# A hybrid pooling and attention backbone on one core: the pool layer's first stage with pinned VectorE and ScalarE orders

## The chip, the cores and the metric

The kernel runs on one core of a Trainium2 chip. A core has a tensor engine (TensorE, PE) that multiplies matrices and writes to PSUM, a vector engine (VectorE, DVE), a scalar engine (ScalarE, ACT), a small general engine (GpSimd, POOL) and a sync engine (SyncE, SP), whose queue here issues every DMA. Each engine works through its own instructions in their order and waits at one whose inputs are not there.

The metric is the device time of one execution in microseconds. One further execution was recorded by the hardware profiler; its views are called the profile, or the trace.

## The reference

A backbone of two layers over 512 latent tokens (with 256 context tokens beside them), width 1024, float32. Layer 0 mixes tokens by centred mean pooling, layer 1 by attention; an MLP with squared ReLU follows each. What matters here is the beginning, the pool half of layer 0:

```python
def ada_mods(cond, w, b):
    m = (jax.nn.silu(cond) @ w + b)[..., None, :]
    return jnp.split(m, N_MOD, axis=-1)          # SH1, SC1, GT1, SH2, SC2, GT2

def pool_mixer(h, w_pool, pool_scale):           # h = rms_norm(x) * g * (1 + SC1) + SH1
    for g, w in enumerate((2, 4, 8, 16)):        # 4 groups of 256 channels
        mean = (jnp.take(csg, hi, axis=1) - jnp.take(csg, lo, axis=1)) / cnt
        diff = (mean - hf[..., sl]).astype(h.dtype)
        outs.append(diff @ w_pool[g])
    return jnp.concatenate(outs, axis=-1) * pool_scale

x = x + gt1 * rms_norm(y_lat, g_mix_post[i])
m_lat = sq_relu_mlp(modulate(rms_norm(x, g_mlp_pre[i]), sh2, sc2), w_mlp_in[i], w_mlp_out[i])
x = x + gt2 * rms_norm(m_lat, g_mlp_post[i])
```

The same is done for the context tokens with their own conditioning vector. The conditioning matrix of a layer, w_ada, is 1024 x 6144 float32; attention later scales q and k by the gains g_q and g_k.

## The kernel before

Tokens stand in six tiles of 128 rows (four latent, two context, `NT` = 6), channels in eight blocks of 128 (`KT` = 8). Float32 operands of the large matmuls are split into a high part that TensorE takes at its fast rate and a low rest, and three products (high x high, high x low, low x high) are added in PSUM.

The first stage, up to the MLP's first long run of matmuls, is made of these pieces; the names are functions in the code.

- `rows_a`, `rows_b`: RMS norm of each token tile; ACT squares, POOL takes the root, DVE scales into `acc`.
- `band_mm`, `band_ev`: the pooling means less identity as matmuls with a banded matrix, into PSUM (`psm` latent, `psc` context). Channel blocks 0 to 3 are copied to two SBUF tiles (`stage`), blocks 4 to 7 stay in PSUM.
- Conditioning, in fourteen items (`CONDITIONING`): a wide item covers 512 columns of one of the six vectors and takes two loads of 1 MB from w_ada, a narrow one covers 256 and takes one load, twenty loads in all. `ada_mm` loads and multiplies (eight matmuls whose four column groups of 32 hold partial sums, tile `psada`), and in the same step DVE transposes the rows in blocks of 32. For a wide item the transposed rows go into the loaded tile itself (`raw[:, 0, :]`). `ada_sel` then turns and sums them with small matmuls (`sel`), and DVE adds the bias and forms the scale vector (`avec`) or the negative of the shift (`minus`). The loads use four slots (pool `rawe`).
- `pool_weights`, `pool_scaled`, `split`: the 1 MB of pool weights is loaded, the 1024 values of pool_scale are copied by DMA to all 128 partitions, DVE multiplies them in, and one whole-tile cast (ACT) and subtraction (DVE) make high and low part.
- `centred(k)`: for one channel block, ACT makes the high part of mean x scale (latent, then context), DVE the low part. This needs SC1 and SH1 of that block.
- `pool_a`, `pool_ms`, `pool_b`: the pool matmuls of a token tile (6 per group, 24 in all, tile `pspool`), the mean square, and the product with the gate.
- `gate_rows`: GT1 times a gain is spread over the partitions by matmuls with the identity (`psg`), in two halves.
- `norm_r`, `norm_s`, `norm_c`, `turn0`, `mod0`, `Inner.part`: residual, second norm, transposes to channel-major, modulation with SC2 and SH2, and the first MLP matmuls (`psin`).

What sets the order: each call stands in a list with a time (`st.at(time, function, ...)`), and the list is run in order of these times. What the engines then execute is decided by a planner of the language, which may move instructions between its costs, except for those that are pinned. Pinned instructions of an engine stay in program order among themselves. The class `Kept` pins everything that goes through it while its switch is on. Before the change only TensorE goes through `Kept`, up to time 50.4 of the list; the loads of `raw_load` on SP are pinned by `raw_load` itself. In the profile every instruction that is pinned by `Kept` has line 65.

Two further lines matter. `head_gains` (line 986) loads g_q and g_k for the attention, spread over all partitions, and multiplies one of them by a constant on DVE. It is called from the MLP's block 4, far behind the first stage, but nothing pins it, and the planner issued both DMAs among the first on SP, with the multiply on DVE between the transposes of the first two conditioning items:

```python
        sy.dma_start(grow[:, 0, :], g_q[0].partition_broadcast(P))
        sy.dma_start(grow[:, 1, :], g_k[0].partition_broadcast(P))
        ve.tensor_scalar(out=grow[:, 0, :], in0=grow[:, 0, :], scalar1=float(HD) ** -0.5, ...)
```

Of the kernel before, what the change touches and what calls it, by code (L numbers as in the profile page):

```python
# [17 lines left out]
P = 128  # L18
# [50 lines left out]
def backbone(ctx: ExitStack, tc, x, ctx_in, w_ada, w_pool, pool_scale, w_qkv, g_q, g_k, w_o, w_mlp_in,  # L69
             w_mlp_out, vecs, rope, band, out):  # L70
    nc = tc.nc
    ordered = [False]
    sy, ve, sc, gp, te = nc.sync, nc.vector, nc.scalar, nc.gpsimd, Kept(tc, nc.tensor, ordered)
# [133 lines left out]
    sy.dma_start(vec, vecs[:, 0:160])  # L207
    sc.activation(cond[:, :, 0:2].rearrange("p k c -> p c k"), given.rearrange("p (c k) -> p c k", k=KT),
# [5 lines left out]
    def ada_mm(i, m, j, w=2):  # L214
        ps = psB.tile([P, 512], F32, tag="b", name="psada")
        kn = 2048 // (w * P)
        for z in range(KT // kn):
            raw = raw_load(w_ada[i, m, j + z]).rearrange("p (k n) -> p k n", n=w * P)
            for k in range(kn):
                at = kn * z + k  # L220
                q = 32 * (at % 4)
                te.matmul(ps[q:q + 32, 0:w * P], cond[:, at, :], raw[:, k, :], start=(at < 4), stop=(at >= 4))
        rows = raw[:, 0, :] if w > 2 else small.tile([P, 256], F32, tag="rows", name="rows", bufs=3)
        ve.transpose(rows, ps[:, 0:w * P])
        rowsd[i, m, j] = ps, rows, w
# [53 lines left out]

    def ada_at(st, t, i, m, j, w=2):  # L280
        st.at(t, ada_mm, i, m, j, w)
        st.at(t + 1, ada_sel, i, m, j)
# [136 lines left out]
    def band_ev(k, q, on_act):  # L419
        if k not in stage:  # L420
            z = rawp.tile([P, 2048], F32, tag="raw", name="stage")
            stage[k] = z[:, 0:2 * TOK].rearrange("p (u n) -> p u n", n=TOK), z[:, 2 * TOK:]
        t0, ln = SEGS[q]
        (sc.copy if on_act else ve.tensor_copy)(stage[k][0][:, :, t0:t0 + ln], (lat, con)[q][k])
        if q:
            for u in range(2):
                means[k + u] = [stage[k][0][:, u, t0:t0 + ln] for t0, ln in SEGS]
# [9 lines left out]
    def centred(k):  # L437
        pm = means.pop(k)
        for ci, (t0, ln) in enumerate(SEGS):
            hi, lo, m = hH[:, k, t0:t0 + ln], hL[:, k, t0:t0 + ln], pm[ci][:, 0:ln]  # L440
            sa = avec[0][0][:, k, ci:ci + 1]
            sc.activation(hi, m, AF.Identity, scale=sa, bias=minus[:, k, ci:ci + 1])
            ve.scalar_tensor_tensor(out=lo, in0=m, scalar=sa, in1=hi, op0=ALU.mult, op1=ALU.subtract)
# [7 lines left out]
    def pool_weights():  # L451
        wraw = raw_load(w_pool, rawp)
        w4 = wraw.rearrange("p (g k n) -> p g k n", k=2, n=256)
        for h, (_, spare) in enumerate(stage.values()):
            sy.dma_start(spare, pool_scale[0, 512 * h:512 * h + 512].partition_broadcast(P))
        pw.extend((wraw, wpH, wpL))

    def pool_scaled():
        w4 = pw[0].rearrange("p (g k n) -> p g k n", k=2, n=256)
        for h, (_, spare) in enumerate(stage.values()):  # L460
            ve.tensor_tensor(out=w4[:, 2 * h:2 * h + 2], in0=w4[:, 2 * h:2 * h + 2],
                             in1=spare.rearrange("p (g n) -> p g n", n=256).unsqueeze(2).broadcast_to([P, 2, 2, 256]),
                             op=ALU.mult)
# [245 lines left out]
    for t in range(NT):  # L709
        st.at(4.6 + 1.3 * t, rows_a, t)  # L710
        st.at(6.8 + 1.3 * t, rows_b, t)
# [9 lines left out]
    for t, z in enumerate((8.6, 9.9, 11.3, 13, 14.6, 18.4)):  # L721
        st.at(z, band_mm, t, range(4))
    for q, k, z in ((0, 0, 14.3), (0, 2, 14.3), (1, 0, 19.6), (1, 2, 19.6)):
        st.at(z, band_ev, k, q, k == 0)
    for k in (4, 6):
        z = 16.1 if k == 4 else 23.4
        st.at(z - 0.1, band_open, k)
        for t in range(NL):
            st.at(z + t / 10, band_mm, t, (k, k + 1))
        for t in range(NL, NT):  # L730
            st.at((25.6 if k == 4 else 27) + t / 10, band_mm, t, (k, k + 1))
# [8 lines left out]
    for h in range(2):  # L740
        for ci in range(2):
            st.at((44.8, 49.6)[h] + (0.1, 0)[ci], gate_rows, 0, GT1, ci, (h,))
    order = (4, 5, 0, 1, 2, 3)
    st.at(34.5, pool_a, 4, (0, 1), True)
    st.at(36.7, pool_a, 4, (2,))
    st.at(37.8, pool_a, 5, (0, 1, 2))
    st.at(40.4, pool_a, 4, (3,))
    st.at(40.5, pool_a, 5, (3,))
    for n, t in enumerate(order):
        b = 50.5 + 2.9 * n  # L750
        if n > 1:
            st.at((44.9, 52.6, 55.6, 58.4)[n - 2], pool_a, t)
        st.at(max(b - 0.5, 41.5 + 1.5 * n), pool_ms, t)
# [678 lines left out]
```

## Time and profile before

| | |
|---|---|
| median of 3 runs | 1183.19 us (1181.87 to 1183.25) |
| profiled execution | 1181.75 us, its span 1180.0 us |
| PE busy | 1140.9 us, 97% of the span |
| DVE busy | 938.0 us, 79% |
| ACT busy | 635.1 us, 54% |
| POOL busy | 65.8 us, 6% |
| bytes moved by DMA | 147.84 MB, mean 125 GB/s |
| granted TensorE clock, mean | 0.993 |

Times in the profile are microseconds from the start of the span. A row of the order of time has the start, the time to the end of the last of its instructions, engine, line, operation, result <- operands by name, shape and count; in brackets the idle time of the engine before it, and what ended that. Matmuls overlap, so a busy PE is not a PE at its peak. A DMA's row on SP is its issue, not the transfer.

### The profile page before, as it was taken

The page shows a single profiled execution, that of the slowest core. Times are in us where ns is not written, and L with a number is a line of the kernel's source. Part 1 is how long each engine was busy: PE and PEld are TensorE (multiplying, and loading weights), DVE is VectorE, ACT ScalarE, POOL GpSimd, SP SyncE. Part 2 cuts the span into 40 slices and gives each one's busy share as a digit, 9 for nine tenths or more (in the row PEclk, how much of TensorE's full clock was granted, in tenths as well). Part 3 has the DMA queues.
Part 4 walks back from the last instruction along what each step waited for, and adds up shares of the span by engine and source line. Part 5 has one row for each costly group of instructions (what it writes and reads, how often), then busy time and mean ns, then how long its engine had stood idle before and what let it go on. Part 6 is the DMA issues. An engine that isn't in the chain of part 4 may idle for free. (4 is left out here: it accounts for less than half of the span.)

```text
span 1180.0 us, 15950 instructions
## 1 busy us (share of the span) xinstructions
PE 1140.9 (97%) x6168; PEld 988.1 (84%) x6168; DVE 938.0 (79%) x1536; ACT 635.1 (54%) x1079; POOL 65.8 (6%) x120
## 2 busy tenths in 40 slices
PE   6699999999999999999999999999899999999997
PEld 5469889899889988998887889998888888888886
DVE  3577777989988999897787589977687779778876
ACT  4467654555444455554576377863676346435522
POOL 2020000000000000000131210001100000000001
PEclk9799999999999999999999999999999999999999
DMA  9795122433333334234421201105234124214312
GB/s 353 294 355 213 36 72 107 143 143 143 144 143 135 116 142 144 107 124 151 189 72 58 85 1 37 37 32 201 108 126 177 40 104 143 108 36 143 107 33 110
DMA packets 25802, 147.84 MB, mean 125 GB/s; under 512 B 2816, under 2 KB 5248, under 8 KB 9984
## 3 DMA queue, kind: packets, MB, share of 16 engines
q1 hardware_dynamic: 25728, 146.84, 33.9%
q8 instruction: 48, 0.79, 0.3%
q14 instruction: 26, 0.21, 0.1%
HBM read 139.49 MB, written 7.34 MB: 124 GB/s over the span
## 5 line engine op out<-in xcount | busy, mean ns | idle before, releaser
L787 PE MATMUL pso<-units,rb 128*128 128x512 f32 x1152 | 278.4, 392 | 0.0
L787 PEld LDWEIGHTS pso<-units,rb 128*128 128x128 f32 x1152 | 214.8, 188 | 41.2
L264 DVE SCALAR_TENSOR_TENSOR rows<-raw,cond,rows 128x256 f32<-128x256 f32 x280 | 126.5, 476 | 2.0
L799 DVE TENSOR_TENSOR acc<-acc,pso 128x512 f32<-128x512 f32 x129 | 85.2, 675 | 41.4 <-PE pso L787 41.2
L548 PE MATMUL psin<-ra,rb 128*128 128x512 f32 (+1 forms) x432 | 104.1, 341 | 2.6 <-ACT ra L359 1.6
L891 PE MATMUL pso<-units,pairs 128*128 128x512 f32 x336 | 82.3, 389 | 0.0
L548 PE MATMUL psin<-ra 128*128 128x512 f32 x256 | 80.5, 389 | 0.0
L548 PEld LDWEIGHTS psin<-ra,rb 128*128 128x128 f32 x432 | 70.1, 189 | 12.3 <-ACT ra L359 1.9
L891 PEld LDWEIGHTS pso<-units,pairs 128*128 128x128 f32 x336 | 63.1, 188 | 13.1
L895 DVE TENSOR_TENSOR acc<-acc,pso 128x512 f32<-128x512 f32 x72 | 48.7, 682 | 28.4 <-PE pso L891 28.4
L182 POOL TENSOR_SCALAR ms<-ss 128x1 f32<-128x1 f32 x20 | 10.6, 530 | 998.1 <-ACT junk L169 986.8
L672 PE MATMUL psin<-ra,units 128*128 128x384 f32 x336 | 65.6, 337 | 0.4 <-ACT psin L684 0.4
L672 PE MATMUL psin<-sums,units 128*128 128x384 f32 x336 | 64.1, 337 | 0.0
L672 PEld LDWEIGHTS psin<-ra,units 128*128 128x128 f32 x336 | 59.7, 188 | 4.0 <-ACT psin L684 0.9
L672 PEld LDWEIGHTS psin<-sums,units 128*128 128x128 f32 x336 | 58.9, 188 | 1.6
L144 DVE TENSOR_TENSOR units<-raw,units 128x1024 fp32r<-128x1024 f32 (+2 forms) x49 | 55.2, 1149 | 3.9 <-ACT units L141 3.8
L548 PEld LDWEIGHTS psin<-ra 128*128 128x128 f32 x256 | 48.1, 188 | 10.0
L141 ACT CAST units<-raw 128x1024 fp32r<-128x1024 f32 (+2 forms) x49 | 46.8, 994 | 13.7 <-PE pso L787 9.6
L797 ACT COPY acc<-pso 128x512 f32<-128x512 f32 x48 | 27.1, 587 | 50.0 <-PE pso L787 49.6
L548 PE MATMUL psin<-rb 128*128 128x512 f32 (+1 forms) x144 | 52.8, 367 | 0.2 <-DVE rb L360 0.2
L1034 PE MATMUL psq<-units,ra 128*128 128x512 f32 x216 | 51.7, 392 | 0.0
L548 PE MATMUL psin<-rb,ra 128*128 128x512 f32 x128 | 49.8, 389 | 0.0
(262 smaller groups left out, 2340.7 us busy)
## 6 DMA issues: line engine op xcount, KB each, us to landing
raw<-in_w_ada SPq DMA_DIRECT2D x48, 1024.0 KB, 5.0
raw<-in_w_mlp_in SPq DMA_DIRECT2D x32, 1024.0 KB, 4.9
raw<-in_w_mlp_out SPq DMA_DIRECT2D x32, 1024.0 KB, 5.2
raw<-in_w_qkv SPq DMA_DIRECT2D x6, 1024.0 KB, 4.9
spill<-xr SPq DMA_DIRECT2D x10, 512.0 KB, 4.2
xr<-spill SPq DMA_DIRECT2D x10, 512.0 KB, 6.8
raw<-in_w_o SPq DMA_DIRECT2D x4, 1024.0 KB, 4.9
xr<-in_x SPq DMA_DIRECT2D x4, 512.0 KB, 5.6
```

Of the source, the lines that this page charges most:

```text
L141: a = sc.copy(hi, raw)
L144: b = ve.tensor_tensor(out=lo, in0=raw, in1=hi, op=ALU.subtract)
L182: gp.tensor_scalar(out=ms[:, 0:1], in0=ss[:, parts - 1:parts], scalar1=rest, scalar2=EPS, op0=ALU.add, op1=ALU.add)
L264: ve.scalar_tensor_tensor(out=r, in0=raw[:, k, :], scalar=cond[:, k, c:c + 1], in1=r, op0=ALU.mult, op1=ALU.add)
L548: te.matmul(ps[:, bank, o:o + ln], w[:, k, fs], rhs, start=start, stop=(k == KT - 1 and n == 2), skip_group_check=len(ks) < KT)
L672: te.matmul(bank, w[k], a[k], start=start and k == 0 and m == 0, stop=stop and k == 3 and m == 2, skip_group_check=True)
L787: te.matmul(pss[h][:, 0:cols[h][1]], a[:, f, ts_], w[:, f, cols[h][0]:sum(cols[h])], start=(n == 0 and not seeded[t]), stop=(n == len(seq) ...
L797: sc.copy(d, ps)
L799: ve.tensor_tensor(out=d, in0=d, in1=ps[:, 0:w], op=ALU.add)
L891: te.matmul(ps, a, w, start=(m == 0), stop=(m == len(seq) - 1))
L895: ve.tensor_tensor(out=M[n][:, t], in0=M[n][:, t], in1=ps, op=ALU.add)
L1034: te.matmul(ps, a[:, k, sl], w[:, k % 4, :], start=(k == 0 and n == 0), stop=(k == KT - 1 and n == 2))
```

## The change

VectorE and ScalarE go through `Kept` too, pinned up to time 50.4 of the list; TensorE stays pinned up to 61. `ada_mm` is cut in two, so that the transpose (`ada_rows`) has a time of its own, and a wide item's transposed rows go into a work tile (pool `tmp`, three tiles) in place of the loaded tile. The pool weights are loaded third among the 1 MB loads, and scaled and split in halves, each half's multiply, cast and subtraction with a time of its own among the means. pool_scale arrives as one row of 4 KB at the beginning; two matmuls with a column of ones spread it into PSUM, from where DVE multiplies it in. `centred` is cut into its ACT and DVE part, pool matmuls are listed group by group, and GT1's first item is listed ahead of the last pool group. The DMAs of `head_gains` are pinned, which puts them behind the sixth load of w_mlp_in on SP. What is computed stays the same.

Behind the first stage the instructions are the same; their order differs by small swaps.

```diff
-    ordered = [False]
-    sy, ve, sc, gp, te = nc.sync, nc.vector, nc.scalar, nc.gpsimd, Kept(tc, nc.tensor, ordered)
+    ordered, mixed = [False], [False]
+    sy, gp = nc.sync, nc.gpsimd
+    te, ve, sc = Kept(tc, nc.tensor, ordered), Kept(tc, nc.vector, mixed), Kept(tc, nc.scalar, mixed)
...
     sy.dma_start(vec, vecs[:, 0:160])
+    scale_row = work_tile()[0:1]
+    sy.dma_start(scale_row, pool_scale[0:1])
+    one = sm_tile("sm")
+    ve.memset(one, 1.0)
...
-        rows = raw[:, 0, :] if w > 2 else small.tile([P, 256], F32, tag="rows", name="rows", bufs=3)
+        rowsd[i, m, j] = ps, w
+
+    def ada_rows(i, m, j):
+        ps, w = rowsd[i, m, j]
+        rows = work_tile()[:, 0:512] if w > 2 else small.tile([P, 256], F32, tag="rows", name="rows", bufs=3)
         ve.transpose(rows, ps[:, 0:w * P])
         rowsd[i, m, j] = ps, rows, w
...
-    def centred(k):
-        pm = means.pop(k)
+    def centred(k, part):
         for ci, (t0, ln) in enumerate(SEGS):
-            hi, lo, m = hH[:, k, t0:t0 + ln], hL[:, k, t0:t0 + ln], pm[ci][:, 0:ln]
+            hi, lo, m = hH[:, k, t0:t0 + ln], hL[:, k, t0:t0 + ln], means[k][ci][:, 0:ln]
             sa = avec[0][0][:, k, ci:ci + 1]
-            sc.activation(hi, m, AF.Identity, scale=sa, bias=minus[:, k, ci:ci + 1])
-            ve.scalar_tensor_tensor(out=lo, in0=m, scalar=sa, in1=hi, op0=ALU.mult, op1=ALU.subtract)
+            if part == 0:
+                sc.activation(hi, m, AF.Identity, scale=sa, bias=minus[:, k, ci:ci + 1])
+            else:
+                ve.scalar_tensor_tensor(out=lo, in0=m, scalar=sa, in1=hi, op0=ALU.mult, op1=ALU.subtract)
...
     def pool_weights():
-        wraw = raw_load(w_pool, rawp)
-        w4 = wraw.rearrange("p (g k n) -> p g k n", k=2, n=256)
-        for h, (_, spare) in enumerate(stage.values()):
-            sy.dma_start(spare, pool_scale[0, 512 * h:512 * h + 512].partition_broadcast(P))
-        pw.extend((wraw, wpH, wpL))
-
-    def pool_scaled():
+        for h in range(2):
+            ps = psB.tile([P, 512], F32, tag="b", name="psg")
+            te.matmul(ps, one[0:1, 0:1].broadcast_to([1, P]), scale_row[:, 512 * h:512 * h + 512], start=True, stop=True)
+            pw.append(ps)
+
+    def pool_load():
+        pw[0:0] = raw_load(w_pool, rawp), wpH, wpL
+
+    def pool_scaled(h):
         w4 = pw[0].rearrange("p (g k n) -> p g k n", k=2, n=256)
-        for h, (_, spare) in enumerate(stage.values()):
-            ve.tensor_tensor(out=w4[:, 2 * h:2 * h + 2], in0=w4[:, 2 * h:2 * h + 2],
-                             in1=spare.rearrange("p (g n) -> p g n", n=256).unsqueeze(2).broadcast_to([P, 2, 2, 256]),
-                             op=ALU.mult)
+        ve.tensor_tensor(out=w4[:, 2 * h:2 * h + 2], in0=w4[:, 2 * h:2 * h + 2],
+                         in1=pw[3 + h].rearrange("p (g n) -> p g n", n=256).unsqueeze(2).broadcast_to([P, 2, 2, 256]),
+                         op=ALU.mult)
+
+    def pool_split(h, on_act):
+        raw, hi, lo = (z[:, 1024 * h:1024 * h + 1024] for z in pw[0:3])
+        if on_act:
+            sc.copy(hi, raw)
+        else:
+            ve.tensor_tensor(out=lo, in0=raw, in1=hi, op=ALU.subtract)
...
-    landing = ((19.5, 23.6), (21.5, 25.4), (28.4, 29.7), (30, 31.2), (32.5, 33.6), (35.2, 37.2), (42, 44.5), (47.2, 49.4),
-               (51, 53.2), (55.5, 57.6), (60.5, 61.7), (62.9, 64), (65.2, 66.4), (67.7, 68.8))
-    for (z, zs), (m, j, w) in zip(landing, CONDITIONING):
-        st.at(z, ada_mm, 0, m, j, w)
-        st.at(zs, ada_sel, 0, m, j)
+    landing = ((19.3, 21.4, 22.4), (23.8, 25.9, 27), (27.1, 28.15, 28.7), (28.9, 30.0, 30.5), (31.4, 32.4, 33.4),
+               (33.7, 34.8, 35.2), (38.4, 40.5, 41.3), (45.2, 47.2, 48),
+               (51, 53, 53.8), (55.8, 57.8, 58.6), (60.5, 61.5, 62), (62.9, 63.9, 64.4), (65.2, 66.2, 66.7), (67.7, 68.7, 69.2))
+    for zs, (m, j, w) in zip(landing, CONDITIONING):
+        for z, fn, also in zip(zs, (ada_mm, ada_rows, ada_sel), ((w,), (), ())):
+            st.at(z, fn, 0, m, j, *also)
     st.at(0, ordered.__setitem__, 0, True)
-    st.at(50.4, ordered.__setitem__, 0, False)
+    st.at(0, mixed.__setitem__, 0, True)
+    st.at(50.4, mixed.__setitem__, 0, False)
+    st.at(61, ordered.__setitem__, 0, False)
...
     for k in range(KT):
-        st.at([26.4, 27.5, 28.6, 29.6, 32.2, 33.2, 38.2, 39.2][k], centred, k)
-    st.at(23, pool_weights)
-    st.at(25.3, pool_scaled)
-    st.at(30.5, lambda: split(*pw))
+        st.at([27.4, 28.8, 30.1, 31.4, 32.7, 34, 35.5, 36.8][k], centred, k, 0)
+        st.at([28.6, 29.7, 31.3, 32.5, 33.8, 35.1, 36.7, 37.9][k], centred, k, 1)
+    st.at(19.25, pool_weights)
+    st.at(19.35, pool_load)
+    for h in range(2):
+        st.at((20.2, 22.1)[h], pool_scaled, h)
+        st.at((21.5, 23.4)[h], pool_split, h, True)
+        st.at((23.4, 24.4)[h], pool_split, h, False)
...
-    st.at(34.5, pool_a, 4, (0, 1), True)
-    st.at(36.7, pool_a, 4, (2,))
-    st.at(37.8, pool_a, 5, (0, 1, 2))
-    st.at(40.4, pool_a, 4, (3,))
-    st.at(40.5, pool_a, 5, (3,))
+    for z, t, g in ((30.6, 4, 0), (32.5, 4, 1), (35.4, 4, 2), (36.2, 5, 0), (36.3, 5, 1), (36.4, 5, 2), (40.4, 4, 3), (40.45, 5, 3)):
+        st.at(z, pool_a, t, (g,), t == 4)
...
     def head_gains():
-        sy.dma_start(grow[:, 0, :], g_q[0].partition_broadcast(P))
-        sy.dma_start(grow[:, 1, :], g_k[0].partition_broadcast(P))
+        tc.keep_in_program_order(sy.dma_start(grow[:, 0, :], g_q[0].partition_broadcast(P)))
+        tc.keep_in_program_order(sy.dma_start(grow[:, 1, :], g_k[0].partition_broadcast(P)))
```

Left out are the new times of `rows_b`, `band_mm`, `band_open`, `band_ev`, `gate_rows`, `pool_ms` and of tile 0's pool matmuls, which move by up to 3 in the list (`pool_ms` by more), and the removal of `ada_at`, which nothing calls.

More of the change, by code (lines that the diff above doesn't have):

```diff
@@ L421, in band_ev @@
             z = rawp.tile([P, 2048], F32, tag="raw", name="stage")
-            stage[k] = z[:, 0:2 * TOK].rearrange("p (u n) -> p u n", n=TOK), z[:, 2 * TOK:]
+            stage[k] = z[:, 0:2 * TOK].rearrange("p (u n) -> p u n", n=TOK)
         t0, ln = SEGS[q]
-        (sc.copy if on_act else ve.tensor_copy)(stage[k][0][:, :, t0:t0 + ln], (lat, con)[q][k])
+        (sc.copy if on_act else ve.tensor_copy)(stage[k][:, :, t0:t0 + ln], (lat, con)[q][k])
         if q:
             for u in range(2):
-                means[k + u] = [stage[k][0][:, u, t0:t0 + ln] for t0, ln in SEGS]
+                means[k + u] = [stage[k][:, u, t0:t0 + ln] for t0, ln in SEGS]
     rs, mix, yg, first = {}, {}, {}, []
@@ L722, in backbone @@
         st.at(z, band_mm, t, range(4))
-    for q, k, z in ((0, 0, 14.3), (0, 2, 14.3), (1, 0, 19.6), (1, 2, 19.6)):
+    for q, k, z in ((0, 0, 14.9), (0, 2, 14.9), (1, 0, 19.35), (1, 2, 19.35)):
         st.at(z, band_ev, k, q, k == 0)
     for k in (4, 6):
[L726 to L731, printed above, removed]
@@ L732, in backbone @@
-    for k in range(KT):
-        st.at([26.4, 27.5, 28.6, 29.6, 32.2, 33.2, 38.2, 39.2][k], centred, k)
-    st.at(23, pool_weights)
-    st.at(25.3, pool_scaled)
-    st.at(30.5, lambda: split(*pw))
+        st.at({4: 16, 6: 21.3}[k], band_open, k)
+    for t in range(NL):
+        st.at(16.1 + t / 10, band_mm, t, (4, 5))
+        st.at((21.35, 21.4, 22.6, 22.7)[t], band_mm, t, (6, 7))
+    for t in range(NL, NT):
+        st.at(25.8 + t / 10, band_mm, t, (4, 5))
+        st.at((28.2, 30)[t - NL], band_mm, t, (6, 7))
@@ L751, in backbone @@
         if n > 1:
-            st.at((44.9, 52.6, 55.6, 58.4)[n - 2], pool_a, t)
-        st.at(max(b - 0.5, 41.5 + 1.5 * n), pool_ms, t)
+            st.at((42.5, 52.6, 55.6, 58.4)[n - 2], pool_a, t)
+        st.at((41.6, 42.3, 46, 55.6, 58.6, 61.4)[n], pool_ms, t)
         st.at(b, pool_b, t)
```

10 lines of the change are left out of this document (4 added, 6 removed).

## The prediction

> **What bounds the kernel now.** The page gives TensorE (PE) 97% busy over the span, so I asked where it is not: first the engines' busy time by stage, then the waits of SP's DMA queue, then the order of time up to 111 us. Stages first (length, then busy time and count for PE, weight loads, DVE, ACT, POOL; granted clock, DMA share, GB/s), with six short slices below them.
>
> ```profile
> 20.00:44.00 24.00, 14.63 (x152) 8.62 (x145) 14.94 (x31) 9.15 (x13) 0.00 (x0) 0.79 0.96 383
> 44.00:67.10 23.10, 19.66 (x170) 14.09 (x169) 6.58 (x17) 6.97 (x15) 1.72 (x4) 0.93 0.56 206
> 67.10:107.00 39.90, 38.88 (x384) 31.78 (x383) 34.03 (x59) 30.63 (x59) 9.85 (x20) 1.00 0.81 317
> 22.00:24.00 2.00, 1.37 (x11) 0.53 (x12) 0.00 (x0) 0.00 (x0) 0.00 (x0) 1.00 0.48 125
> 32.00:34.00 2.00, 0.79 (x16) 0.24 (x8) 2.00 (x5) 2.00 (x2) 0.00 (x0) 0.93 0.99 418
> 34.00:36.00 2.00, 0.00 (x0) 0.00 (x0) 2.00 (x6) 0.10 (x1) 0.00 (x0) 0.50 1.04 434
> 46.00:48.00 2.00, 2.00 (x18) 1.13 (x10) 0.45 (x1) 0.00 (x0) 0.00 (x0) 0.66 0.00 0
> 52.00:54.00 2.00, 1.78 (x17) 1.18 (x19) 0.33 (x1) 1.10 (x3) 0.30 (x1) 1.00 0.00 0
> 62.00:64.00 2.00, 1.74 (x16) 0.26 (x8) 0.20 (x1) 0.00 (x0) 0.00 (x0) 1.00 0.29 45
> ```
>
> The first stage ends at 110.68 (row further down), where PE starts its long run of 96 matmuls; behind that it is dense to the end, so whatever the first stage gains is kept. In 20 to 44 the DMA engines are full (0.96) while PE has 14.63 of 24 us. In 44 to 67.1 they are only 0.56 busy, with slices of no traffic at all (46, 52) or little (62). From 67.1 to 107 PE has 38.88 of 39.90 and DVE 34.03: full. The slack is thus in the middle, and SP's queue says who makes it:
>
> ```profile
> SPq L122 <- PE psada L65: 34.0, 12, 7.0
> 41.03 0.33 SPq L122 DMA_DIRECT2D raw<-in_w_ada  x1
> 47.11 0.33 SPq L122 DMA_DIRECT2D raw<-in_w_ada  x1
> 54.53 0.33 SPq L122 DMA_DIRECT2D raw<-in_w_ada  x1
> 62.94 0.33 SPq L122 DMA_DIRECT2D raw<-in_w_ada  x1
> ```
>
> SP waited 34.0 us for PE's conditioning matmuls (psada), which free the four slots of the 1 MB loads of w_ada; I call these loads 1 to 20. Load 11 goes out at 41.03, the next only at 47.11, then 54.53, then 62.94. In order of time:
>
> ```profile
> 22.63 1.06 PE L65 MATMUL psada<-raw,cond 128*32 128x512 f32 x8 [0.99 <-DMA raw<-in_w_ada]
> 25.73 0.23 DVE L989 TENSOR_SCALAR grow<-grow 128x128 f32<-128x128 f32 x1 [4.17 <-DMA grow<-in_g_q]
> 25.87 0.71 DVE L224 STREAM_TRANSPOSE raw<-psada 128x512 f32<-128x512 f32 x1
> 29.11 2.36 DVE L461 TENSOR_TENSOR raw<-raw,stage 128x1024 f32<-128x1024 f32 x2 [1.79 <-DMA raw<-in_w_pool]
> 31.72 1.07 PE L65 MATMUL psada<-raw,cond 128*32 128x256 f32 x16 [2.78 <-DMA raw<-in_w_ada]
> 42.26 2.93 PE L65 MATMUL pspool<-rb,ra 128*128 128x256 f32 x12
> 45.12 1.94 PE L65 MATMUL psada<-raw,cond 128*32 128x256 f32 x16
> 51.85 0.48 DVE L443 SCALAR_TENSOR_TENSOR ra<-psc,avec,ra 128x256 fp32r<-128x256 f32 x1
> 52.38 1.09 PE L65 MATMUL pspool<-rb,ra 128*128 128x256 f32 x7 [0.22 <-DVE ra L443]
> 53.41 1.93 PE L65 MATMUL psada<-raw,cond 128*32 128x512 f32 x16
> 61.81 1.92 PE L65 MATMUL psada<-raw,cond 128*32 128x512 f32 x16
> 65.31 2.05 PE L65 MATMUL psg<-ident,gc 128*128 128x128 f32 x16 [0.48 <-DVE gc L287]
> 70.00 3.13 PE L476 MATMUL pspool<-rb,ra 128*128 128x256 f32 x24
> 110.68 16.91 PE L548 MATMUL psin<-ra,units 128*128 128x384 f32 x96 [0.25 <-ACT work L555]
> ```
>
> One load takes 2.6 us (pool weights landed at 29.11, load 5 at 31.72), 2.4 at the 434 GB/s of the slice from 34: I take 2.5. Load 4 landed at 22.63, but pool weights only 6.5 us later: 2.5 of that is their own, the other 4.0 went to pool_scale and the gains g_q and g_k, spread over partitions by DMA (the slice from 22 moved 125 GB/s). DVE stood 4.2 us before the multiply of g_q (25.73), and the transpose of SH1's first rows was queued behind it. Then PE: the matmul of SH1's last load (45.12) stood behind pool matmuls, ran at half clock (1.94 against 1.07 at 31.72), and with it came late the last centred half (ends 52.33), the pool matmuls of the last group (52.38), GT1's two conditioning items (53.41, 61.81) and the second gate broadcast, which ends at 65.31 + 2.05 = 67.36. From there to 110.68 are 43.3 us, in which PE is full. **67.36 is my milestone**: what it moves, the end moves.
>
> **The change part by part.** Durations, from one execution:
>
> ```profile
> 18.85 2.78 PE L65 MATMUL psada<-raw,cond 128*32 128x512 f32 x24
> 23.62 1.71 PE L65 MATMUL psm<-gate,acc 128*128 128x136 f32 x12
> 25.27 0.25 PE L65 MATMUL psada<-raw,sel 128*32 128x8 f32 x8
> 26.82 2.12 PE L65 MATMUL psc<-gate,acc 128*128 128x136 f32 x16
> 27.42 4.90 ACT L442 ACTIVATE ra<-stage,phase,avec 128x512 fp32r<-128x512 f32 x8 [8.33 <-DVE phase L244]
> 31.39 4.31 DVE L443 SCALAR_TENSOR_TENSOR ra<-stage,avec,ra 128x512 fp32r<-128x512 f32 x8
> 35.99 2.25 DVE L144 TENSOR_TENSOR rb<-raw,rb 128x2048 fp32r<-128x2048 f32 x1
> 41.55 0.44 DVE L224 STREAM_TRANSPOSE rows<-psada 128x256 f32<-128x256 f32 x1
> 67.12 1.29 DVE L321 TENSOR_TENSOR acc<-pspool,gate 128x512 f32<-128x512 f32 x2 [1.79 <-ACT gate L300]
> 68.33 2.47 DVE L324 SCALAR_TENSOR_TENSOR xr<-acc,rs,xr 128x1024 f32<-128x1024 f32 x2
> 105.97 3.89 ACT L141 CAST units<-raw 128x1024 fp32r<-128x1024 f32 x4
> 107.05 3.50 DVE L144 TENSOR_TENSOR units<-raw,units 128x1024 fp32r<-128x1024 f32 x3 [0.26 <-ACT units L141]
> ```
>
> A float32 matmul leaves two records (the 8 matmuls of a narrow conditioning item stand as x16), so: wide item 1.93, narrow 1.07, column turn (sel) 0.25, band matmuls of two channel blocks over the 256 context tokens about 1.1, 24 pool matmuls 3.1 (12 of them 2.93 at half clock), a centred block 1.23 on ACT (4.90/4) and 1.08 on DVE (4.31/4).
>
> *Removed:* the 0.5 MB of pool_scale and, from this place, g_q and g_k: 4.0 us for every load behind them. Their four issues on SP go too; its queue runs ahead of the landings, so that is worth nothing by itself. The pool weights move ahead of load 3, so load 4 lands at 25.1 rather than 22.6, load 5 at 27.6, load 8 at 35.1, load 10 at 40.1, load 12 at 45.1, as long as slots come free in time.
>
> *pool_scale spread by PE:* a DMA of one row, issued ahead of load 1, whose matmul began at 18.85, so it is there by then; a memset on DVE before there is any data; two float32 matmuls of 512 columns, unseen here. By the gate broadcast (8 matmuls of 128 columns in 2.05) 512 columns are 4 x 0.256 = 1.0 each; the lower end is 0.24 (four 512-wide conditioning matmuls side by side take 1.93/2), the upper 1.6 (six band matmuls of some 140 columns in 1.71, so 1.05 for 512, and half as much again because one row is an odd shape). I take 1.0, the same kind of work: 2.0 us on PE ahead of the first conditioning item, which ran from 18.85. Ends: 1.5 us earlier, 1.2 later.
>
> *Pool weights scaled and split amid the means:* scaling 1.2 to 1.3 per half on DVE; casts of half size 0.97 on ACT (3.89/4), 1.17 on DVE (3.50/3). Same work as the 2.36 and 2.25 above, but at 21 to 28, when DVE otherwise waits for loads; the 2.25 at 35.99 no longer stands before the second narrow item's sums.
>
> *Transposed rows in work tiles, transposes placed apart:* the slot of a wide load is free after its matmul, not after transpose and turn. That is 1 to 3 us per wide load, hidden where DMA is full; it counts through loads 13 to 16 only.
>
> *Pinned orders:* the walk along each engine's order in the changed program, at full clock:
> - PE: 18.9 spread, 20.9 SC1 (wide), 22.9 band, turn, band to 25.3, SH1 (wide) to 27.3, band context 28.4, turn 28.6.
> - DVE: scale half 0 20.9 to 22.2, transpose SC1 22.9 to 23.6, half 1 24.9, sums 25.3, two low splits 27.6, transpose SH1 28.3, sums and minus 28.9. ACT starts the centred halves at 28.95 (before: 27.42) and has blocks 0 to 3 by 33.9.
> - Now each narrow item costs DVE 0.44 + 0.35 between centred blocks: blocks 0 and 1 end at 32.7, SH1's second item at 33.8, block 2 34.9, transpose 35.65, block 3 36.75. Here DVE waits: the next sums need a turn that PE has behind the pool matmuls of block 3 (37.5): 37.8 to 38.2. Blocks 4, 5 and the last transpose: 40.8; last shift 41.2. ACT blocks 6, 7: 43.75; DVE 44.3 (before 52.33).
> - PE: 24 pool matmuls 40.85 to 43.95; GT1 wide item, now ahead of the last pool group, 45.9; last group 47.4; turn and gate columns 48.2; broadcast 50.25; pool matmuls of tile 0 53.35; GT1's second item 55.3; transpose, turn, columns 56.8; broadcast **58.85**.
>
> Gain at the milestone: 67.36 - 58.85 = 8.5. The waits that take the place of the old ones are DVE's own queue (by these durations 19 of the 23.4 us from 20.9 to 44.3 are work) and the transpose of SC2, which two residual updates now precede; the turn behind it is pinned ahead of the next pool matmuls on PE: 0.9 lost. SP is ready: load 13 goes out when GT1's first half is through (45), 15 at 54.4, 19 near 68.5, each at least 5 us before its use.
>
> *g_q and g_k later:* pinned directly behind a w_mlp_in load in the steady state, read by DVE right after that load's first use. Alone, 64 KB of short rows land some time behind the 1 MB: 0 to 1.5 us of DVE wait, of which I take 0.3, nearer the lower end, since they are a sixteenth of the load ahead of them.
>
> Sum: 8.5 - 0.9 - 0.3 = 7.3. The profiled execution took 1181.75 (span 1180.0 and 1.75 around it), giving 1174.45; the median of the runs is 1.44 higher, giving **1175.9**.
>
> **The rivals.**
> *Half clock again (0.22).* Before, the slice from 34 has clock 0.50: it had begun to fall in the slice from 32 (0.93), after PE had worked 0.79 of those 2 us, and in the slice from 46 (0.66) it had not long been up again: some 13 us. In my walk PE has its thinnest stretch from 32 to 41, 4.4 us of work in 9 and no gap over 1.6. Against the drop: no slice of 2 us without work; for it: the narrow items use a quarter of the array. If it falls, the 24 pool matmuls cost 3.0 more and of the 0.9 more of the last narrow item 0.7 comes through: gain 7.3 - 3.7 = 3.6, 1179.6. The Trainium skill ("TensorE: Matmul & The Clock Gate", section "HAM oscillation — how this bites in real kernels") says to have no PE-idle gap over about 3.4 us; by it the clock stays full and the time is 1175.9; before, it began to fall after a gap of 2.8 us (the wait in the row at 31.72) and a burst of 1.07, so the trace shows the rule to be a little too kind.
>
> *Nearer to the ends of the estimate (0.12).* If the spread costs 0.24 each and the turns come when DVE is free, SH1's minus is there at 27.5 and DVE's waits at 36.75 vanish: 1.5 + 1.0 more, and the full stage behind the milestone loses its PE idle of some 2 to 3 us: gain about 12, 1171.
>
> *Nothing (0.06).* The stage behind the milestone also asks 34.0 us of DVE and 30.6 of ACT in 39.9. If their order there, which is not pinned, leaves PE waiting for what it would have waited for anyway, the end stays: 1183.
>
> *Slower (0.09).* PE stays pinned longer than DVE and ACT. Six turns in that stage stand in PE's order ahead of pool, transpose or MLP matmuls, each waiting for a DVE transpose that now queues behind residuals (2.47/2) and products (1.29/2). At 2 us each it is 12 us of idle PE: 1183.2 - 8.2 + 12 = 1187. It decides once PE's idle time behind the milestone passes some 10 us; in the rows before, PE stood for 1 of 39.9, and the same turns were there.
>
> **How the numbers follow.** The forecast has 0.51, from 1173.5 to 1178. The range 1170.5 to 1180.8 adds the first two rivals and leaves out nothing and slower, 0.15, with a little of each tail. Within 0.2% (2.4 us, about what a measurement here can tell from no change) fall nothing and the late part of the clock rival: 0.10. Faster 0.81, slower 0.09.
>
> **What would show it.** Right: no g_q wait on DVE before 30; pool weights split by about 28; centred halves beginning near 29; last one near 44; second broadcast ending near 59; the 96 matmuls starting near 103; clock 1.00 from 30 to 45. Wrong: a clock of 0.50 there; a spread of 3 us or more; PE idle over 3 us between 59 and 103; SP still waiting long for psada at loads 11 to 13; a changed time behind 110 us, above all a DVE wait for g_q of over 2 us.

## The result, and the profile after

The changed kernel takes 1185.54 us (median; 1182.24 to 1187.64), the kernel before beside it 1182.76 us (1181.43 to 1185.21). The ratio is 1.0019, with an interval of 1.0012 to 1.0027: slower by 2.8 us in the medians and 2.2 by the ratio, where 7.3 us less was forecast, and outside the range. (The ratio is not exactly the quotient of the two medians.) The profiled execution took 1186.68 us, its span 1184.9 us, at a mean granted clock of 0.991 (before 0.993).

The milestone of the prediction, the end of the second gate broadcast, did move: to 59.28 + 2.05 = 61.33 from 67.36, a gain of 6.0. But the run of 96 matmuls starts at 115.55 and not at 110.68. Two windows show it, first of the kernel before, cut at its milestone and at the start of its 96 matmuls (length, then busy time and count for PE, weight loads, DVE, ACT, POOL; clock, DMA share, GB/s):

```profile
20.00:67.36 47.36, 34.54 (x324) 22.85 (x320) 21.76 (x49) 16.12 (x28) 1.72 (x4) 0.86 0.76 297
67.36:110.68 43.32, 42.05 (x409) 34.86 (x409) 37.42 (x63) 34.31 (x64) 9.85 (x20) 1.00 0.76 292
```

Then of the kernel after, cut at the same two events:

```profile
20.00:61.33 41.33, 34.94 (x334) 23.68 (x336) 22.48 (x50) 17.49 (x33) 2.58 (x6) 0.92 0.82 327
61.33:115.55 54.22, 46.86 (x409) 39.18 (x409) 37.04 (x62) 31.71 (x58) 11.16 (x18) 0.87 0.61 230
```

Both stages hold the same 409 matmuls. Before, PE needed 42.05 us for them and stood for 1.3; after, it needs 46.86, at a clock of 0.87, and stands for 7.4. So the stage is 4.8 us longer by the clock and 6.1 by idle time: 10.9 together, against the 6.0 won ahead of it. Behind the start of the 96 nothing changed: 1180.0 - 110.68 = 1069.3 us before, 1184.9 - 115.55 = 1069.4 after.

The waits of PE in that stage of the kernel after (in all, times, longest):

```profile
PE psin L65 <- ACT ra L395: 3.2, 1, 3.2
PE psx L65 <- ACT acc L521: 3.1, 1, 3.1
PE psin L65 <- DVE ra L396: 1.0, 1, 1.0
```

And the order of time that makes them (PE, DVE, ACT and POOL in one list):

```profile
18.51 1.98 PE L65 MATMUL psg<-work,sm 1*128 1x512 f32 x4
29.16 0.17 DVE L65 TENSOR_TENSOR phase<-mods 128x8 f32<-128x8 f32 x1
40.90 5.49 PE L65 MATMUL pspool<-rb,ra 128*128 128x256 f32 x24 [0.96 <-DVE ra L65]
44.22 0.48 DVE L65 SCALAR_TENSOR_TENSOR ra<-psc,avec,ra 128x256 fp32r<-128x256 f32 x1
46.31 2.05 PE L65 MATMUL psada<-raw,cond 128*32 128x512 f32 x16
59.28 2.05 PE L65 MATMUL psg<-ident,gc 128*128 128x128 f32 x16 [0.48 <-DVE gc L65]
69.61 2.29 DVE L145 TENSOR_TENSOR rb<-raw,rb 128x2048 fp32r<-128x2048 f32 x1 [0.43 <-ACT rb L142]
70.71 1.27 POOL L177 TENSOR_SCALAR ms<-ss 128x1 f32<-128x1 f32 x1 [1.88 <-ACT junk L170]
71.29 0.33 PE L65 MATMUL psx<-ident,acc 128*128 128x128 f32 x1
71.82 1.28 DVE L329 SCALAR_TENSOR_TENSOR xr<-acc,rs,xr 128x1024 f32<-128x1024 f32 x1
72.06 1.46 POOL L185 TENSOR_TENSOR rs<-ms,nhalf 128x1 f32<-128x1 f32 x1
73.56 1.15 ACT L521 ACTIVATE acc<-xr,rs 128x1024 f32<-128x1024 f32 x1 [1.44 <-POOL rs L185]
74.76 0.90 PE L65 MATMUL psx<-ident,acc 128*128 128x128 f32 x3 [3.14 <-ACT acc L521]
75.31 5.47 PE L65 MATMUL pspool<-rb,ra 128*128 128x256 f32 x24
75.84 0.22 POOL L177 TENSOR_SCALAR ms<-ss 128x1 f32<-128x1 f32 x1 [1.27 <-ACT junk L170]
76.14 0.57 POOL L185 TENSOR_TENSOR rs<-ms,nhalf 128x1 f32<-128x1 f32 x1
80.88 0.60 ACT L170 ACTIVATE junk<-pspool 128x512 bf16<-128x512 f32 x1 [5.13 <-PE pspool L65]
82.18 1.01 ACT L389 ACTIVATE acc<-psx,mods,avec 128x256 f32<-128x256 f32 x2
84.12 0.62 ACT L395 CAST ra<-acc 128x512 fp32r<-128x512 f32 x1
84.79 0.58 PE L65 MATMUL psin<-ra,rb 128*128 128x256 f32 x1 [3.24 <-ACT ra L395]
89.00 1.94 PE L65 MATMUL psada<-raw,cond 128*32 128x256 f32 x16
115.55 16.81 PE L562 MATMUL psin<-ra,units 128*128 128x384 f32 x96
```

TensorE's order is now written out up to time 61 of the list, and in it the second transpose of the first MLP block (psx, 74.76) stands ahead of the pool matmuls of tile 3 (75.31). It needs the normed tile that ACT makes at 73.56, and that was late: POOL's two one-column operations before it took 1.27 and 1.46 us. So 24 matmuls whose operands were ready stood behind a transpose for 3.1 us. Meanwhile ACT ran dry: its next instruction squares the result of just those matmuls (80.88, after 5.1 us of waiting), and only behind that come the modulation (82.18) and the cast (84.12) for which PE's next pinned matmul then waits 3.2 us (84.79). The two engines wait for each other in turn. After each of the two long gaps PE runs at half clock for a while: the 24 pool matmuls take 5.47 us, not 3.13, and the narrow conditioning item at 89.00 takes 1.94, not 1.07.

### The profile page after: what moved, and what is told of

Same layout as the page of the kernel before. It is cut to its first block, busy times and chain, and to the rows that moved or that the text cites. A ratio compares the mean times of both kernels' runs of the same rounds, so it can differ in the third digit from the quotient of the medians.

```text
span 1184.9 us, 15958 instructions
## 1 busy us (share of the span) xinstructions
PE 1146.2 (97%) x6172; PEld 993.3 (84%) x6172; DVE 938.6 (79%) x1538; ACT 636.2 (54%) x1080; POOL 67.5 (6%) x120
## 5 line engine op out<-in xcount | busy, mean ns | idle before, releaser
L142 ACT CAST units<-raw 128x1024 fp32r<-128x1024 f32 (+2 forms) x49 | 46.8, 994 | 14.3 <-PE pso L807 10.2
```

Source lines behind the costliest of these rows:

```text
L142: a = sc.copy(hi, raw)
```

## The experiments

For each kernel the table gives the milestone, the start of the 96 matmuls, PE's busy and idle time between the two and the clock there, all of its one profiled execution, then the median of its timed runs and their ratio to those of the kernel before on the same chip. Kernels are compared by this ratio: E1 to E4, E5 to E8 and E9 to E12 stood beside runs of before with medians of 1182.36, 1183.23 and 1182.77, so medians compare directly only within these groups. "No pin" is said of VectorE and ScalarE; before has TensorE pinned to 50.4 and no other pin.

| kernel | milestone | 96 start | PE busy + idle | clock | median us | ratio (interval) |
|---|---|---|---|---|---|---|
| before | 67.36 | 110.68 | 42.05 + 1.27 | 1.00 | 1182.76 | 1 |
| after: PE to 61, DVE and ACT to 50.4 | 61.33 | 115.55 | 46.86 + 7.36 | 0.87 | 1185.54 | 1.0019 (1.0012 to 1.0027) |
| E1: after, PE to 50.4 | 58.61 | 105.45 | 44.85 + 1.99 | 0.93 | 1178.41 | 0.9968 (0.9955 to 0.9981) |
| E2: before, PE to 61 | 66.24 | 116.78 | 45.46 + 5.08 | 0.93 | 1188.96 | 1.006 (1.0043 to 1.0077) |
| E3: before, g_q and g_k late | 66.55 | 110.90 | 41.92 + 2.43 | 1.00 | 1180.40 | 0.9982 (0.9972 to 0.9991) |
| E4: after, PE to 57.9 | 61.09 | 110.02 | 44.41 + 4.52 | 0.93 | 1179.36 | 0.9977 (0.9967 to 0.9986) |
| E5: after, all three to 61 | 62.00 | 120.53 | 46.97 + 11.56 | 0.88 | 1190.41 | 1.0057 (1.0039 to 1.0076) |
| E6: after, PE to 50.4, no pin | 58.14 | 102.74 | 42.90 + 1.70 | 1.00 | 1175.57 | 0.9937 (0.9922 to 0.9952) |
| E7: E1 with pool_scale by DMA | 62.04 | 110.49 | 44.89 + 3.56 | 0.93 | 1180.76 | 0.9976 (0.9967 to 0.9986) |
| E8: E1 with rows in the loaded tile | 60.00 | 106.77 | 43.64 + 3.13 | 0.96 | 1178.23 | 0.9966 (0.9953 to 0.9979) |
| E9: after, PE to 61, no pin | 58.52 | 110.29 | 44.15 + 7.62 | 0.93 | 1182.41 | 0.9993 (0.9983 to 1.0002) |
| E10: E6 with g_q and g_k early | 60.14 | 105.56 | 42.53 + 2.89 | 1.00 | 1175.72 | 0.9938 (0.992 to 0.9955) |
| E11: after, no engine pinned | 58.11 | 106.26 | 45.22 + 2.93 | 0.91 | 1177.18 | 0.9951 (0.9936 to 0.9966) |
| E12: E6 once more | 59.80 | 104.39 | 42.89 + 1.70 | 1.00 | 1173.45 | 0.992 (0.9905 to 0.9935) |

The theory from the profile after: TensorE's longer pin makes the stage behind the milestone wait, and the waits bring the half clock. The rival: the order of VectorE and ScalarE there is at fault, and PE's gaps are only where it shows.

**E1, TensorE's pin back to where it ended before.**

```diff
-    st.at(61, ordered.__setitem__, 0, False)
+    st.at(50.4, ordered.__setitem__, 0, False)
```

> The changed kernel with TensorE's written order ended at 50.4 instead of 61; nothing else. Theory A (the longer pin of TensorE): behind the second gate broadcast TensorE stood 3.1 + 3.2 + 1.0 us for pinned transposes and turns and lost some 4 us more to half clock; with them free both go, the run of 96 matmuls starts near 104 to 106 instead of 115.55, and the time falls by 9 to 11 us, to a ratio near 0.993 against before. Theory B (the order of VectorE and ScalarE behind the milestone; TensorE's gaps are only its symptom): the run of 96 still starts within 2 us of 115.5 and the time stays at 1.000 to 1.002.

The waits of PE between milestone and 96 matmuls:

```profile
PE psada L227 <- DVE mods L249: 1.2, 1, 1.2
PE psx L379 <- ACT acc L521: 0.6, 1, 0.6
56.56 2.05 PE L65 MATMUL psg<-ident,gc 128*128 128x128 f32 x16 [0.48 <-DVE gc L65]
105.45 16.81 PE L562 MATMUL psin<-ra,units 128*128 128x384 f32 x96
```

One line brings the time from 1.0019 to 0.9968, some 6 us. The waits of 3.1, 3.2 and 1.0 are gone, 1.2 and 0.6 have come. The start of the 96 is as the theory had it; the ratio, 0.9968, is not as far down as its 0.993. The profile flatters E1: its profiled execution, 1176.74, is the shortest of its five (to 1180.25), and that of after lies 1.1 above its median. In E1's profile the clock still falls in this stage (0.93); the longer executions have lower mean clocks (0.993 to 0.994 against 0.996), but where they lost it no profile shows. With the first part at full clock the milestone stands at 56.56 + 2.05 = 58.61, where the prediction's walk had 58.85.

**E2, the same edit the other way, in the kernel before.**

```diff
-    st.at(50.4, ordered.__setitem__, 0, False)
+    st.at(61, ordered.__setitem__, 0, False)
```

> The kernel before with TensorE's written order extended from 50.4 to 61; nothing else. Theory A: TensorE gets waits of 3 us or more between 67 and 111 there too, the run of 96 starts past 114 and the time rises by 4 to 10 us (ratio 1.003 to 1.009). Theory B: within 1 us of before (ratio 0.999 to 1.001).

```profile
66.24:116.78 50.54, 45.46 (x409) 36.51 (x409) 37.47 (x63) 33.06 (x62) 11.76 (x20) 0.93 0.65 248
PE psin L548 <- ACT ra L390: 3.0, 1, 3.0
PE pspool L65 <- DVE acc L321: 1.4, 1, 1.4
```

The pin alone costs the kernel before 0.6%: the milestone is there as early as ever (66.24), yet the 96 start 6.1 us later, with 3.0 us of waiting for the same cast by ACT and a clock of 0.93. The rival, no change, falls.

**E4, which of the pinned instructions.** The pin ends just ahead of the first MLP block's transposes and matmuls; conditioning items, turns and pool matmuls up to there stay in written order.

```diff
-    st.at(61, ordered.__setitem__, 0, False)
+    st.at(57.9, ordered.__setitem__, 0, False)
```

> The changed kernel with TensorE's written order ended at 57.9: the transposes and the MLP matmuls of the first tile of that run are free, the conditioning items, turns and pool matmuls up to there stay in written order. Theory A with all of the loss in the freed instructions: as with the end at 50.4, within 1.5 us (ratio near 0.993). Theory A with the turns and conditioning items holding TensorE as well: between, 0.995 to 0.999. Theory B: 1.000 to 1.002.

```profile
PE psada L227 <- DVE mods L249: 3.0, 1, 3.0
PE psada L238 <- DVE mods L249: 1.5, 1, 1.5
```

Most comes back with these few instructions freed: 0.42% (1.0019 to 0.9977) of E1's 0.51%, and the intervals of the two overlap. What remains in this profile are waits of PE for the DVE operation that empties a conditioning bank, and both stand at instructions that are no longer pinned (lines 227 and 238).

**E5, all three engines pinned to the same place.** If the harm came from TensorE being pinned further than the other two, as the prediction's slower rival put it, this would cure it.

```diff
-    st.at(50.4, mixed.__setitem__, 0, False)
+    st.at(61, mixed.__setitem__, 0, False)
```

> The changed kernel with the written order of VectorE and ScalarE extended from 50.4 to 61, so that all three engines are pinned to the same place. Theory A1 (the loss is a mismatch: TensorE stands in written order while the scheduler lets VectorE and ScalarE do other work first): TensorE's waits of 3.1 and 3.2 us behind the second gate broadcast fall under 1.5 us each, the run of 96 starts near 108 to 111, ratio 0.995 to 0.999. Theory A2 (TensorE's written order asks for these operands too early, in whatever order the other two work): the waits stay above 2 us each, the run of 96 stays past 113, ratio 1.000 to 1.003.

```profile
62.00:120.53 58.53, 46.97 (x410) 38.77 (x410) 38.89 (x64) 31.84 (x58) 8.04 (x18) 0.88 0.58 221
PE pspool L65 <- DVE acc L65: 5.6, 2, 3.5
PE psin L65 <- ACT junk L170: 5.1, 1, 5.1
```

It does not; it costs 0.4% more. PE stands for 11.6 us, 5.6 of it for a DVE result that is now pinned (L65) and 5.1 for ACT's squares. So it is not a mismatch: the written order asks for operands before they exist, and a second engine bound to it adds waits of its own.

**E6 and E12, TensorE pinned to 50.4 and nothing else; E9, TensorE to 61 and nothing else; E11, nothing pinned.** Against after, E6 drops the two lines that pin VectorE and ScalarE and ends TensorE's pin early; E9 drops only the two lines; E11 drops all pins.

```diff
-    st.at(0, mixed.__setitem__, 0, True)
-    st.at(50.4, mixed.__setitem__, 0, False)
-    st.at(61, ordered.__setitem__, 0, False)
+    st.at(50.4, ordered.__setitem__, 0, False)
```

> The changed kernel with TensorE's pin ended at 50.4 and with no pin on VectorE and ScalarE at all. If these pins carry the first stage, the scheduler's order makes the last centred half and with it the second gate broadcast 2 to 5 us later than 58.6: ratio 0.998 to 1.001. If the order is the same without them, as with the pins: 0.996 to 0.998, the broadcast within 1 us.

> The changed kernel with TensorE's pin to 61 as in the change, and no pin on VectorE and ScalarE. If TensorE's long pin costs by itself, whatever the other two do: TensorE again waits 5 us or more in all behind the second gate broadcast, ratio 0.999 to 1.004, some 0.6 to 0.9% above the version with the pin ended at 50.4 and no other pin (0.9937). If the long pin hurts only together with pinned VectorE and ScalarE: 0.993 to 0.996.

> The changed kernel with no pin on any engine. If TensorE's written order carries the first stage, the second gate broadcast ends 2 us or more later than 58.14 and the ratio is 0.996 to 1.003. If the scheduler finds as good an order from the listed times: 0.992 to 0.995.

> The same kernel as the one with TensorE's pin ended at 50.4 and no pin on VectorE and ScalarE, for its interval and for how often the clock falls: 0.9925 to 0.995, runs between 1173 and 1178 us, the time going with the run's mean granted clock (about 1173.5 at 0.999, 1176 at 0.996).

Windows of E6 (up to its milestone, and from there to the 96 matmuls):

```profile
20.00:58.14 38.14, 32.11 (x334) 21.27 (x336) 21.78 (x50) 17.69 (x33) 2.58 (x6) 1.00 0.88 354
58.14:102.74 44.60, 42.90 (x409) 35.19 (x410) 37.10 (x62) 31.50 (x58) 9.91 (x18) 1.00 0.72 279
```

The same two of E12:

```profile
20.00:59.80 39.80, 33.85 (x334) 22.77 (x336) 21.77 (x50) 17.69 (x33) 2.58 (x6) 0.96 0.86 340
59.80:104.39 44.59, 42.89 (x410) 35.17 (x409) 37.10 (x62) 31.50 (x58) 9.91 (x18) 1.00 0.72 281
```

E9, its second window and the waits of PE in it:

```profile
58.52:110.29 51.77, 44.15 (x410) 36.26 (x410) 37.33 (x62) 31.71 (x58) 9.63 (x18) 0.93 0.63 241
PE psin L65 <- ACT ra L395: 6.7, 1, 6.7
PE psx L65 <- ACT acc L521: 0.8, 1, 0.8
```

With no pin on VectorE and ScalarE the milestone comes no later (58.14, expected 2 to 5 us later): the planner finds as good an order, so these pins, which gave the change its name, carry nothing. The time falls to 0.9937 and, the second time, 0.992, which beats both kernels. What the VectorE and ScalarE pins cost (E1 against E6 and E12, 0.3 to 0.5%) is only in part explained. Between the profiles of E1 and E6 it is 0.5 us at the milestone, 0.3 of idle time and 2.0 of PE busy time, since the clock fell in E1's stage (0.93) and not in E6's. At the same mean clock, 0.996, E1 took 1176.74 and 1178.01 and E6 1176.16 and 1176.29, so 0.5 to 1.9 us are left beside the clock. Why the clock is lower with the pins, no run shows. E9 leaves TensorE's long pin alone, and its wait is still there, 6.7 us for the same cast. Four of the kernels thus make a square: TensorE's pin to 61 instead of 50.4 costs 0.5% with the other pins (1.0019 against 0.9968) and 0.6 to 0.7% without (0.9993 against 0.9937 and 0.992). E11 suggests that TensorE's pin up to 50.4 is worth keeping, by 0.14 to 0.31% (0.9951 against 0.9937 and 0.992); its interval overlaps that of E6, though, so this is not settled. Its milestone is as early (58.11), so the pin does not carry the first stage either; the loss is in the stage behind, at a clock of 0.91.

**E3 and E10, the loads of g_q and g_k.** E3 moves them late in the kernel before, E10 lets them out early in the best version. The edit is the change's own:

```diff
-        sy.dma_start(grow[:, 0, :], g_q[0].partition_broadcast(P))
+        tc.keep_in_program_order(sy.dma_start(grow[:, 0, :], g_q[0].partition_broadcast(P)))
```

> The kernel before with only the two loads of g_q and g_k moved into the steady state. Their wait of 4.2 us on VectorE and some 1 to 2 us of transfer ahead of load 5 go. If the first stage is bound by its loads, the second gate broadcast ends 1 to 3 us earlier than 67.36 and the time falls by as much (ratio 0.998 to 0.999); if the later place costs a wait of its own in the steady state, the time rises; if neither, no change (1.000).

> The changed kernel with TensorE's pin ended at 50.4, no other pin, and the loads of g_q and g_k free to go out in the first stage as before. If their transfers and the wait of VectorE behind them cost what the prediction's loads term says (1.5 to 2 us of the 4.0), the second gate broadcast ends 1.5 to 2.5 us later than 58.14: ratio 0.995 to 0.996. If they are hidden: 0.993 to 0.9945.

The wait of E10's first part, and its second broadcast:

```profile
PE psada L65 <- DMA raw<-in_w_ada: 2.0, 1, 2.0
58.09 2.05 PE L65 MATMUL psg<-ident,gc 128*128 128x128 f32 x16 [0.48 <-DVE gc L292]
```

E3 gains 2.0 us in the median (1180.40 against 1182.36 beside it), as expected; its profile does not show where, since the profiled execution, at 1183.08, was the longest of its range: the milestone is 0.8 earlier, and a load comes 1.2 us late in the stage behind. In E10 the two loads make PE wait 2.0 us for a conditioning load, and the milestone comes 2.0 later than in E6, as expected. The ratio does not show it: 0.9938 lies where it was expected if the loads were hidden, beside 0.9937 and 0.992 without them. At the same mean clock of 0.999 E10 took 1175.19 and 1175.36, E6 and E12 from 1173.28 to 1173.62, a price of 1.8 us, from two and four executions. DVE did not wait for g_q here; but behind the wait of 2.0 the clock fell (0.50 from 30 to 32), so the profile does not part the transfer from the clock.

**E7 and E8, the other two parts, undone in E1.** E7 copies pool_scale to all partitions by two DMAs behind the pool weights; E8 puts the transposed rows of wide items back into the loaded tile.

```diff
-            ps = psB.tile([P, 512], F32, tag="b", name="psg")
-            te.matmul(ps, one[0:1, 0:1].broadcast_to([1, P]), scale_row[:, 512 * h:512 * h + 512], start=True, stop=True)
+            sy.dma_start(pw[3 + h], pool_scale[0, 512 * h:512 * h + 512].partition_broadcast(P))
...
-        rows = work_tile()[:, 0:512] if w > 2 else ...
+        rows = raw[:, 0, :] if w > 2 else ...
```

> The changed kernel with TensorE's pin ended at 50.4, and pool_scale spread over partitions by two DMAs of 0.25 MB behind the pool weights as before, instead of by two matmuls. If the spread by DMA costs transfer time in the first stage, load 4 lands 1 to 2 us later and the second gate broadcast ends 1 to 2.5 us later: ratio 0.998 to 0.999. If TensorE's two matmuls cost as much as they save (2.0 us ahead of the first conditioning item), no difference from the version with them: 0.996 to 0.998.

> The changed kernel with TensorE's pin ended at 50.4, and the transposed rows of the wide items put back into the landing slot of the load. If slots set when loads 13 to 16 land, GT1's second item begins 1 to 2 us later and the time rises by as much: ratio 0.998 to 0.999. If loads are ahead by then, as the prediction has it: within 0.5 us, ratio 0.996 to 0.998.

The waits of PE in E7's first part:

```profile
PE psada L65 <- DVE work L65: 3.8, 2, 2.8
PE pspool L65 <- DVE ra L65: 1.8, 2, 1.0
```

pool_scale by DMA costs 3.4 us at the milestone, more than expected there. DVE's scaling waited 3.1 us for its load (22.90), the transpose pinned behind it came late, PE waited 2.8 us for that, and the clock fell in that wait: 0.92 up to the milestone (E1: 1.00). But E7's profiled execution is the longest of its ten and E1's the shortest of its five. By the ratio the cost is 0.08%, some 0.9 us, and the intervals overlap; against E8, timed beside E7, it is 0.1% or 2.5 us of median. So the spread by matmuls seems worth its place, but by how much stays open, and it was compared only with DVE's order pinned. The work tiles are worth nothing that can be told here (0.9966 against 0.9968).

## Why the prediction was wrong

*The step that failed* is "67.36 is my milestone: what it moves, the end moves", with the sentence before it, "From there to 110.68 are 43.3 us, in which PE is full". PE was full there in the order that the planner had chosen. The change writes that order out, up to 61, and with it the stage takes 54.2 us. The prediction listed the pins, walked every engine to the milestone and stopped there; of the pinned instructions behind it only the SC2 turn got a price (0.9). E1, E2 and E9 show the pin to be the cause. One of the prediction's own signs of being wrong, "PE idle over 3 us between 59 and 103", came true: PE stood for 7.4 us there, up to the 96 matmuls.

*Its slower rival* had the right place, "PE stays pinned longer than DVE and ACT", with a price of 12 us and a chance of 0.09. Its time, 1187, came near the 1185.54 by other waits. It counted six turns, of which only the first two (66.19 and 80.71 in the profile after) stand ahead of 61 in the list and are pinned, and these waited for nothing; the transposes and the first MLP matmuls waited instead. And the row held against it, "in the rows before, PE stood for 1 of 39.9, and the same turns were there", was no evidence: before, nothing pinned them. E5 also takes away its reason: pinned to the same place, all three are slower still.

*The half-clock rival* came true in the profiled execution: 24 pool matmuls began at half clock at 40.90, and the milestone was 61.33, 2.5 us behind the walk; 3.7 was the price given. PE worked for 6.2 us from 32 to 41, more than the 4.4 of the walk, and the clock fell all the same. The chance of 0.22 looks low: with the first stage of the change as it is, these 24 matmuls took 5.49 us in three profiles (after, E4, E5) and 3.13 in one (E1). At full clock (E1, 58.61; E6, 58.14) the walk, 58.85, was right to 0.7 us. By the rule cited from the Trainium skill ("TensorE: Matmul & The Clock Gate", section "HAM oscillation — how this bites in real kernels") it should not have fallen: the longest wait of PE from 33 to 41 was 1.0 us. The trace disagrees with the rule here.

*Point by point.* The spread by matmuls: 2.0 forecast, 1.98 measured (18.51). SH1's minus: 28.9 forecast for its end, 29.33 measured (the row at 29.16, where its tile is called phase). The last centred half: 44.3 forecast, 44.70 measured. GT1's wide item: 45.9 forecast at its end, 48.4 with the half clock. The loads: g_q and g_k 2.0 at the milestone (E10; only 0.8 in the kernel before, E3), pool_scale 3.4 (E7), with the clock's part in both; 4.0 was given to the two together. The later place of g_q and g_k: 0.3 forecast, a choice without a row behind it, and nothing measured (1069.3 and 1069.4 us behind the start of the 96). The stage without the long pin: 43.3 + 0.9 forecast, 44.6 measured (E6, E12) and 46.8 with the pins on VectorE and ScalarE (E1). E6 and E12 together ran from 1173.28 to 1176.29, around the forecast of 1175.9; but that is another kernel, without the pinned orders to which the prediction gave its gain. E1, which has them, took 1178.41, so the agreement with E6 and E12 is in part luck.

## What to carry to other kernels

A stage in which an engine is full is full in the order it ran in; when a change also fixes that order, the walk has to go on through every pinned instruction, asking of each whether its operand exists by then, until the pin ends. Pin one engine, no further than the stage where the planner errs, and test the end of the pin by itself: it is one number, and here it cost 0.51% where the rest of the change had won 0.32% (E1). A pin that is expected to carry a gain is worth one run without it: E6 was the better kernel. At full clock a walk by the durations of one profile came within 0.7 us at the milestone; what a moved load is worth came out less surely, 0.8 and 2.0 us at the milestone for the same two.

## What the runs showed of the hardware

*The clock falls in one execution of a program and not in another.* E6 and E12 are one kernel, on two chips. From 20 to the milestone its clock was 1.00 in one profile and 0.96 in the other, with nearly the same idle time of PE (6.03 and 5.95 us), and the milestone differed by 1.7 us. On one chip E6's four executions have mean clocks from 0.996 to 0.999. Of the kernel after, the execution with a mean clock of 0.990 took 1187.64 us, those at 0.996 took 1182.24 and 1182.51: its spread goes with the clock. At the same 0.996 E1 took 1176.74 and 1178.01, so the long pin costs some 4 to 6 us beside what it does to the mean clock. These slices show, for after, a fall with no wait of PE over 1.0 us and, for E9, no fall in 2 us without any work (length, then as above):

```profile
36.00:38.00 2.00, 0.95 (x13) 0.53 (x11) 1.31 (x4) 0.00 (x0) 0.00 (x0) 1.00 1.05 422
38.00:40.00 2.00, 1.32 (x24) 0.57 (x24) 1.91 (x5) 1.11 (x2) 0.00 (x0) 0.95 0.95 389
40.00:42.00 2.00, 1.10 (x5) 1.10 (x6) 1.12 (x5) 0.98 (x3) 0.00 (x0) 0.50 1.00 418
74.00:76.00 2.00, 0.00 (x0) 0.00 (x0) 1.68 (x5) 1.97 (x5) 1.05 (x3) 1.00 1.04 303
76.00:78.00 2.00, 0.00 (x0) 0.00 (x0) 2.00 (x3) 1.96 (x5) 1.81 (x3) 0.88 0.94 293
```

In after (the first three rows) PE was busy for 0.95 and 1.32 of two slices of 2 us, the second with narrow conditioning and turn matmuls alone, and the clock began to go before 40. E1, whose first stage is the same, had 0.90 and 1.12 us in these two slices and kept 1.00. In E9 (the last two rows) PE stopped at 73.80 and the clock was still full through 76. So no length of gap decides by itself in these runs. The same page of the Trainium skill, section "Part 1: The HAM clock gate", says that the window in which activity is judged runs freely, so that the point of a change varies from run to run; after and E1, and E6 and E12, agree with that, while the window itself shows in no trace here.

*POOL's small operations stretched beside VectorE.* The operation on one column of 128 (line 177) took 0.22 us at 75.84 in the profile after, and the next (line 185) 0.57. In the rows at 70.71 and 72.06 they took 1.27 and 1.46 (the profile's times on POOL are rough), while DVE ran operations with two SBUF inputs (69.61 to 71.90, 71.82 to 73.10). The first ended 0.1 us behind the first of these, the second 0.4 behind the second. The Trainium skill ("SBUF — State Buffer", section "SBUF: two separate sides") says that such a DVE operation, if it starts first, holds a port which POOL also reads through, and that POOL then waits; the trace agrees. By the durations at 75.84 and 76.14 they would have ended some 1.9 us earlier (an estimate), most of the 3.1 us for which PE waited at the transpose. In E9 that wait was only 0.8, and PE then waited 6.7 for the cast: less of the one does not lessen the whole.
